# A 2112-byte pitch between the tiles of activations and gated products, and the memory's squares summed on VectorE

## The chip, the cores and the metric

The kernel runs on one core of a Trainium2 chip. The metric is the device time of one execution in microseconds; several executions are made and their median is given. A profile is one further execution, recorded instruction by instruction. The engines are TensorE (PE in the profile, with its weight loads as PEld), VectorE (DVE), ScalarE (ACT), GpSimd (POOL) and SyncE (SP, which issues most loads).

## The reference

A two-layer decoder trunk on 256 positions of width 1024 (float32). Each layer is: half-step SwiGLU, a mixer, half-step SwiGLU.

```python
def swiglu(x, w_gate, w_up, w_down):
    return (jax.nn.silu(x @ w_gate) * (x @ w_up)) @ w_down

for layer in range(2):
    if layer == 1:
        shared_kv = shared_moba_kv(h, ...)           # one key/value set, from the stream
    h = h + 0.5 * swiglu(rms_norm(h, ffn1_g), ...)   # D_FF = 2816
    hn = rms_norm(h, mix_g)
    # layer 0: 31-tap convolution module on 768 channels, layer 1: causal attention (12 heads);
    # both beside 4-head attention over a memory of 256 rows:
    mem_out = memory_attention(q_mem, rms_norm(mem, mem_g), w_mem_kv, ...)
    h = h + concat([primary, mem_out]) @ w_o
    h = h + 0.5 * swiglu(rms_norm(h, ffn2_g), ...)
```

The memory is normalized by its own root mean square, `rstd(mem)`, before its keys and values are projected.

## The kernel before

**Layout.** Activations stand transposed: 128 partitions are 128 of the 1024 (or 2816) channels, the 256 positions lie along the row. A float32 product is made of float32r parts: an activation is split into a high part and a low part, a weight as well, and of the four products three are summed: high weight by high and by low activation, low weight by high activation. The tile of split activations (`y_tiles`, pool `yp`) is `[128, 8, 2, 256]`: for each of the 8 blocks k of channels the high part and then the low part, 2048 bytes in all. The gated products `hs` (pool `hp`) are `[128, 22, 2, 256]` in the same way. So a 512-column matmul takes both parts of one k in one go with the high weight (`wh`), and a 256-column matmul takes the high part with the low weight (`wl`); `mm_run` lists these. Weights come in chunks of 1 MB, two halves each; ScalarE makes `wh` of a half (line 182), VectorE makes `wl` as raw minus `wh` (line 186), four buffers of 4096 bytes for each. One weight tile is 512 bytes of a row, so k moves on by 2048 bytes in the activations and by 512 in the weights.

**The stages.** `ffn` is called four times, with the names a, b, c, d. Its first loop runs over 22 blocks j of D_FF: gate (`ag`) and up (`au`) sums in PSUM, 32 matmuls a step in full flow, then scaling, Silu and product into `hs`. Its second loop runs over 8 blocks m of the output (`ao`, `bo`, `co`, `do`). Between them are the input projections, the attention stages, `kv` (keys and values shared by layer 1, where activations are the standing operand and `wh`, `wl` move), and the output projections `oao` and `obo`.

**The order of the work.** A scheduler places instructions; `ffn` takes a `hook(j)` that is called at the start of step j > 1 and whose instructions are kept behind the last weight split of the step before. In the first `ffn` the hook is `prepare`: at j == 5 it loads the memory `mT` and small tables, works out the rotary angles, and at its end sums the squares of the memory: `square_sum` makes the square of block k on ScalarE (`mq1` to `mq7`, two buffers) and adds it to `macc` on GpSimd (line 285), one block after another. `rstd_cols` then makes the column sums with two tiny matmuls (`rm_p`), adds epsilon on VectorE (`rm_v`) and takes the power on GpSimd (`rm_`); VectorE copies the result to `rm`. At j == 9 (`MEM_AT`) the hook scales and splits the memory (`my`, ScalarE and VectorE) and projects it (`mkv`); `rm` is used when those sums are read (`mk0t`, `mv`).

An engine takes its instructions in order, so what stands behind `rm_p` in TensorE's queue waits for it. Names in the profile are those of the tiles, with numbers left out where they repeat. A float32 matmul is recorded as two.

Of the kernel before, what the change touches and what calls it, by code (L numbers as in the profile page):

```python
# [9 lines left out]
F32 = mybir.dt.float32  # L10
F32R = mybir.dt.float32r
BF16 = mybir.dt.bfloat16
I32 = mybir.dt.int32
AF = mybir.ActivationFunctionType
ALU = mybir.AluOpType
AX = mybir.AxisListType

P = 128
DM = 1024
KD = DM // P  # L20
SEQ = 256
NT = SEQ // P
DFF = 2816
KF = DFF // P
# [26 lines left out]
MEM_AT = 9  # L51
FIRST_CAT = 3
TURN_AT = 2
Q_AT = 6
CNR_AT = 4

# [27 lines left out]
def tile_kernel(ctx: ExitStack, tc: tile.TileContext, w, xT, memT, pos, vec, hg, const, out):  # L84
    nc = tc.nc
    yp = ctx.enter_context(tc.tile_pool(name="yp", bufs=2))
    cp = ctx.enter_context(tc.tile_pool(name="cp", bufs=1))
    wp = ctx.enter_context(tc.tile_pool(name="wp", bufs=3))
    tp = ctx.enter_context(tc.tile_pool(name="tp", bufs=2))
    op = ctx.enter_context(tc.tile_pool(name="op", bufs=4))  # L90
    hp_ = ctx.enter_context(tc.tile_pool(name="hp", bufs=1))
# [8 lines left out]
    mT = cp.tile([P, KD, SEQ], F32, name="mT", tag="t8k")  # L100
# [148 lines left out]
        return ps.tile([P, 512], F32, name=name, tag=tag, bufs=bufs)  # L249


    def y_tiles(name):
        return yp.tile([P, KD, 2, SEQ], F32R, name=name, tag="y")

    def y_both(name):
        whole = yp.tile([P, KD, 2, SEQ], F32, name=name + "w", tag="y")
        return y_tiles(name), whole[:, :, 0]

    def scaled_split(y, src, k, g, on_dve=False):
# [19 lines left out]
    def square_sum(name, acc, src, first, adder=nc.gpsimd):  # L279
        if first:  # L280
            nc.scalar.activation(acc, src, AF.Square)
        else:
            sq = tp.tile([P, SEQ], F32, name=name, tag="sq")
            nc.scalar.activation(sq, src, AF.Square)
            adder.tensor_tensor(acc, acc, sq, op=ALU.add)

    def mean_cols(name, acc):

        pr = psum(name + "p", "aux", 2)
        for i in range(NT):  # L290
            mmul(pr[:, i:i + 1], acc[:, i * P:(i + 1) * P], onec, start=True, stop=True)
        v = tp.tile([P, NT], F32, name=name + "v", tag="rv")
        nc.vector.tensor_scalar(v, pr[:, :NT], EPS, None, op0=ALU.add)
        state["stat"] = state["last"]["P"]
        return v

    def rstd_cols(name, acc):
        v = mean_cols(name, acc)
        r = tp.tile([P, NT], F32, name=name, tag="rc", bufs=3)
        nc.gpsimd.tensor_tensor(r, v, mhalf[:, :NT], op=ALU.pow)  # L300
        return r
# [22 lines left out]

    def ffn(name, y, acc, nexts, store=False, both=False, hook=None, after=None, hook_down=None):

        hs = hp_.tile([P, KF, 2, SEQ], F32R, name=name + "hs", tag="hs")
        rb, first = None, acc is None
        for j in range(KF):
            if hook and j > 1:  # L330
# [3 lines left out]
            if first and j == 0:  # L334
# [12 lines left out]
                sq = cp.tile([P, KD, SEQ], F32, name="sq0", tag="kv")  # L347
                for k in range(KD):
                    nc.scalar.activation(sq[:, k], x[:, k], AF.Square)
                n = KD  # L350
# [28 lines left out]
            s = tp.tile([P, SEQ], F32, name=f"{name}s{j}", tag="s")  # L379
# [76 lines left out]
    def proj(name, y, *uses):  # L456

        os_ = [psum(f"{name}{t}") for t in range(NT)]
        n = MW * len(uses)
        if isinstance(y, tuple):  # L460
            raw = raw_chunk()
            for k in range(KD):
                for t in range(NT):
                    mmul(os_[t][:, :n], y[1][:, k, t * P:(t + 1) * P], raw[:, k * n:(k + 1) * n],
                         start=k == 0, stop=k == KD - 1)
        else:
            per = HC // n
            for k0 in range(0, KD, per):
                wh, wl = half_chunk()
                for t in range(NT):  # L470
                    for i in range(per):
                        k = k0 + i
                        mm3_tok(os_[t][:, :n], wh, wl, y, t, k, slice(i * n, (i + 1) * n), k == 0, k == KD - 1)
        for t in range(NT):
            for i, use in enumerate(uses):
                use(t, os_[t][:, i * MW:(i + 1) * MW])
# [24 lines left out]
    def values(name, r, dst, col0):  # L501
        def use(t, o):
            nc.scalar.activation(dst[:, t, col0:col0 + MW], o, AF.Copy, scale=r[:, t:t + 1])
        return use
# [110 lines left out]
    def go(head, n):  # L615
        for _ in range(n):
            next(head)

    def mem_prep(layer):
        y = y_tiles(f"my{layer}")  # L620
        for k in range(KD):
            scaled_split(y, mT[:, k], k, V_MEM + layer * KD)
        return y

    def mem_kv(layer, y, rm):
        kT = cp.tile([P, 2, SEQ], F32, name=f"mk{layer}", tag="mk")
        v = cp.tile([P, NT, MW], F32, name=f"mv{layer}", tag="mv")
        proj(f"mkv{layer}", y, keys(f"mk{layer}", rm, G_MK + layer, kT, 0, False), values(f"mv{layer}", rm, v, 0))
        return kT, v
# [58 lines left out]
    y = y_tiles("y0")  # L688
# [4 lines left out]
    def prepare(j):  # L693
        if j == MEM_AT:
            my = mem_prep(0)
            kv0.extend(mem_kv(0, my, rm))
        if j != 5:
            return
        nc.sync.dma_start(vt[:, V_TAP:], vec[:, V_TAP:])
        nc.sync.dma_start(pt, pos)  # L700
        nc.sync.dma_start(gt, hg)
        nc.sync.dma_start(mT, memT)
        nc.vector.tensor_copy(identb, ident)
        nc.vector.tensor_tensor(ident2, ident[:, :HALF_CH], ident[:, HALF_CH:], op=ALU.add)
        nc.vector.tensor_copy(maskb, cst[:, C_MASK:C_MASK + P])

        for g, n in ((G_MQ, 2), (G_Q, 1)):
            gn = gt[:, g * HD:(g + n) * HD]
            nc.vector.tensor_scalar(gn, gn, -1.0, None, op0=ALU.mult)

        posf = cp.tile([P, NT], F32, name="posf")
        nc.vector.tensor_copy(posf, pt)
        ang = cp.tile([P, NT, HALF], F32, name="ang")
        for i in range(NT):
            nc.vector.tensor_scalar(ang[:, i], cst[:, C_FREQ:C_FREQ + HALF], posf[:, i:i + 1], None, op0=ALU.mult)
        for shift, dst in ((0.25, cosT), (0.0, sinT)):
            kk = tp.tile([P, NT, HALF], F32, name="kk", tag="kk")
            nc.vector.tensor_scalar(kk, ang, 1.0 / TWO_PI, shift, op0=ALU.mult, op1=ALU.add)
            nc.vector.tensor_scalar(kk, kk, ROUND, ROUND, op0=ALU.add, op1=ALU.subtract)
            rr = tp.tile([P, NT, HALF], F32, name="rr", tag="rr")  # L720
            nc.vector.scalar_tensor_tensor(rr, kk, -PI_1, ang, op0=ALU.mult, op1=ALU.add)
            nc.vector.scalar_tensor_tensor(rr, kk, -PI_2, rr, op0=ALU.mult, op1=ALU.add)
            nc.vector.scalar_tensor_tensor(rr, kk, -PI_3, rr, op0=ALU.mult, op1=ALU.add)
            if shift:
                nc.vector.tensor_scalar(rr, rr, TWO_PI / 4, None, op0=ALU.add)
            nc.vector.tensor_scalar(rr, rr, 3.1415925, -3.1415925, op0=ALU.min, op1=ALU.max)
            nc.scalar.activation(dst[:, :, HALF:], rr, AF.Sin)
            if shift:
                nc.vector.tensor_copy(dst[:, :, :HALF], dst[:, :, HALF:])
            else:  # L730
                nc.vector.tensor_scalar(dst[:, :, :HALF], dst[:, :, HALF:], -1.0, None, op0=ALU.mult)

        macc = tp.tile([P, SEQ], F32, name="macc", tag="macc", bufs=1)
        for k in range(KD):
            square_sum(f"mq{k}", macc, mT[:, k], k == 0)
        nc.vector.tensor_copy(rm, rstd_cols("rm_", macc))

    identb = cp.tile([P, P], BF16, name="identb")
    maskb = cp.tile([P, P], BF16, name="maskb")
# [2 lines left out]
    rm = cp.tile([P, NT], F32, name="rm")  # L742
# [4 lines left out]
    def diagonals(m):  # L747
        for i in range(m * 4 * SHIFTS // KD, (m + 1) * 4 * SHIFTS // KD):
            g, s, p = i // (2 * SHIFTS), i // 2 % SHIFTS, i % 2
            nc.scalar.activation(diag[:, g, s, p * HALF_CH:(p + 1) * HALF_CH], ident2, AF.Copy,  # L750
                                 scale=vt[:, V_PP + i:V_PP + i + 1])

    (y,), acc = ffn("a", y, None, (V_MIX,), both=True, hook=prepare, after=AF.Sigmoid, hook_down=diagonals)

    hc = hp_.tile([P, KF * 2 * SEQ], F32, name="hc", tag="hs")
    hp = hc[:, :CC * (PAD + SEQ)].rearrange("p (c s) -> p c s", c=CC)
    whole = hc[:, CC * (PAD + SEQ):CC * (PAD + SEQ) + 2 * SEQ].rearrange("p (i s) -> p i s", i=2)
    cv = hc[:, KF * SEQ:KF * SEQ + CC * SEQ].rearrange("p (c s) -> p c s", c=CC)
# [151 lines left out]
    for c in range(CC):  # L910
        V(nc.vector.tensor_tensor(cv[:, c], cv[:, c], mean, op=ALU.subtract))
        sq = hp[:, c, PAD:]
# [69 lines left out]
    for k, (wh, wl, *_) in enumerate(halves):  # L982
        for m in range(KD):
            s = slice(m * P, (m + 1) * P)
# [7 lines left out]
    for m in range(KD):  # L992
        for k in range(FIRST_CAT, CC):
            mm3(o[m], next(it), cat, k, False, k == CC - 1, skip_group_check=True)
        out_end(m, o, ys, acc, V_FFN2, "oa")
    y = ys
    (ykv, y), acc = ffn("b", y, acc, (V_KV, V_FFN1 + KD))


# [11 lines left out]
    mq = qT[:, NPAIR:]  # L1011
# [14 lines left out]
    n = len(pairs)  # L1026
    for p in range(n + 1):
        if p < n:
            go(pairs[p], 1)
        if p == TURN_AT:  # L1030
            for turn in turns:
# [14 lines left out]
    y, acc = next(oproj)  # L1046
# [4 lines left out]
def _pack_weights(np_, d):  # L1051
# [20 lines left out]
    def cols(m, n=NB):  # L1072
        chunks(blocks(m, n))
# [26 lines left out]
    q = parts.pop()  # L1100
    parts.append(np_.concatenate([up[:Q_AT], q, up[Q_AT:]], axis=0))
    cols(d["w_mem_kv"][1])
# [71 lines left out]
```

## Time and profile before

| | |
|---|---|
| median of three executions | 985.27 us (983.53 to 986.44) |
| the profiled execution | 989.74 us, span 988.0 us from first to last instruction |
| mean granted clock of TensorE | 0.993 |
| TensorE busy | 973.2 us, 5788 records |
| VectorE / ScalarE / GpSimd busy | 744.2 / 599.8 / 135.7 us |
| loads from HBM | 171.43 MB, 175 GB/s over the span |

A busy time is the union of an engine's instructions. Matmuls are pipelined: each is recorded longer than the distance to the next one, so the time of one in a stream is read from start to start. The granted clock is the share of full speed at which TensorE was allowed to run. The waits list names the engine that waited, the line, and what ended the wait.

### The profile page before, as it was taken

To read this page: it belongs to the slowest core of one execution; us is meant where nothing else is said; L and a number is where in the kernel's file an instruction comes from. 1 tells how busy PE (TensorE), PEld (TensorE's weight loads), DVE (VectorE), ACT (ScalarE), POOL (GpSimd) and SP (SyncE) were. 2 spreads that over 40 slices of the span, in tenths; PEclk is the share of its full clock that TensorE was granted. 3 is DMA by queue.
4 is the path that set the end of the run, shared out by engine and by line. 5 is a ranking of instruction groups with operands and counts; after the bars stand their busy time and mean duration, and the time that the engine had idled before them with its cause. 6 is when DMAs were issued, how large, how long until landed. Compare 5 with 4: busy or idle time off the path is not lost.

```text
span 988.0 us, 15410 instructions
## 1 busy us (share of the span) xinstructions
PE 973.2 (99%) x5788; PEld 848.0 (86%) x5788; DVE 744.2 (75%) x1326; ACT 599.8 (61%) x1154; POOL 135.7 (14%) x151
## 2 busy tenths in 40 slices
PE   8899999999999999999999999999999999999998
PEld 6788888898769888888888888888996798888887
DVE  7787776679977888877766787776688588878663
ACT  6576568747667656665546656565556656565542
POOL 0502000118822100000122100000152030000000
PEclk9899999999999999999999999999998999999999
DMA  8545545543225655555555455555552056455560
GB/s 325 207 170 174 207 173 190 194 171 105 109 101 197 212 175 204 177 203 181 176 198 179 171 185 199 180 192 202 194 171 86 1 188 233 177 201 182 185 221 22
DMA packets 26427, 173.47 MB, mean 176 GB/s; under 512 B 3184, under 2 KB 4848, under 8 KB 6000
## 3 DMA queue, kind: packets, MB, share of 16 engines
q1 hardware_dynamic: 26064, 172.31, 49.7%
q8 instruction: 45, 0.74, 0.3%
q14 instruction: 30, 0.25, 0.1%
q10 hardware_dynamic: 288, 0.17, 0.1%
HBM read 171.43 MB, written 1.05 MB: 175 GB/s over the span
## 4 chain that ended last, share of the span: by engine, by line
PE 90%; ACT 3%; DVE 3%; POOL 2%; DMA 1%; issue 1%; SPq 0%; POOLq 0%; ACTq 0%; DVEq 0%
PE cg L149 7%; PE co L149 6%; PE ao L149 6%; PE do L149 6%; PE bo L149 6%; PE dg L149 6%; PE bg L149 6%; PE bu L149 6%; PE du L149 6%; PE cu L149 6%; PE ag L149 6%; PE au L149 5%; PE kv L149 3%; PE oao L149 2%; PE obo L149 2%; PE mkv L149 2%
## 5 line engine op out<-in xcount | busy, mean ns | idle before, releaser
L186 DVE TENSOR_TENSOR wl<-raw,wh 128x1024 fp32r<-128x1024 f32 (+1 forms) x310 | 377.3, 1220 | 106.5 <-ACT wh L182 99.6
L182 ACT ACTIVATE wh<-raw 128x1024 fp32r<-128x1024 f32 (+1 forms) x310 | 322.9, 1046 | 129.4 <-PE do L149 20.6
L149 PE MATMUL ag<-y,wh 128*128 128x512 f32 x176 | 48.6, 406 | 1.1 <-ACT wh L182 1.1
L149 PE MATMUL au<-y,wh 128*128 128x512 f32 x176 | 46.8, 393 | 0.0
L149 PE MATMUL co<-chs,wh 128*128 128x512 f32 (+1 forms) x198 | 45.5, 367 | 0.0
L149 PE MATMUL bo<-bhs,wh 128*128 128x512 f32 (+1 forms) x198 | 45.5, 367 | 0.0
L149 PE MATMUL do<-dhs,wh 128*128 128x512 f32 (+1 forms) x198 | 45.5, 367 | 0.0
L149 PE MATMUL ao<-ahs,wh 128*128 128x512 f32 (+1 forms) x198 | 45.4, 367 | 0.0
L149 PE MATMUL bg<-oay,wh 128*128 128x512 f32 x176 | 44.9, 393 | 0.0
L149 PE MATMUL cg<-by,wh 128*128 128x512 f32 x176 | 44.3, 393 | 0.3 <-DVE cgs L239 0.3
L149 PE MATMUL dg<-oby,wh 128*128 128x512 f32 x176 | 44.5, 393 | 0.0
L149 PE MATMUL bu<-oay,wh 128*128 128x512 f32 x176 | 44.4, 392 | 0.0
L149 PE MATMUL du<-oby,wh 128*128 128x512 f32 x176 | 44.4, 392 | 0.0
L149 PE MATMUL cu<-by,wh 128*128 128x512 f32 x176 | 44.3, 393 | 0.0
L835 POOL TENSOR_TENSOR hc<-hc,cq 128x256 f32<-128x256 f32 x58 | 42.5, 734 | 12.5 <-ACT cq L834 8.7
L843 DVE SCALAR_TENSOR_TENSOR cvp<-hc,vt,cvp 128x256 f32<-128x256 f32 x88 | 40.6, 484 | 1.5
L149 PEld LDWEIGHTS ag<-y,wh 128*128 128x128 f32 x176 | 34.1, 195 | 8.8 <-ACT wh L182 1.5
L149 PEld LDWEIGHTS ao<-ahs,wh 128*128 128x128 f32 x198 | 35.0, 189 | 5.4
L149 PEld LDWEIGHTS cg<-by,wh 128*128 128x128 f32 x176 | 32.9, 188 | 7.7 <-DVE cgs L239 0.8
L149 PEld LDWEIGHTS co<-chs,wh 128*128 128x128 f32 x198 | 35.0, 189 | 5.3
L149 PEld LDWEIGHTS bo<-bhs,wh 128*128 128x128 f32 x198 | 34.9, 189 | 5.2
L149 PEld LDWEIGHTS do<-dhs,wh 128*128 128x128 f32 x198 | 34.9, 189 | 5.2
(996 smaller groups left out, 2144.2 us busy)
## 6 DMA issues: line engine op xcount, KB each, us to landing
raw<-in_w SPq DMA_DIRECT2D x158, 1024.0 KB, 4.8
raw<-in_w SPq DMA_DIRECT2D x5, 512.0 KB, 8.3
mT<-in_memT SPq DMA_DIRECT2D x1, 1024.0 KB, 7.9
out<-x SPq DMA_DIRECT2D x8, 128.0 KB, 1.7
raw<-in_w SPq DMA_DIRECT2D x2, 256.0 KB, 4.1
x<-in_xT SPq DMA_DIRECT2D x1, 512.0 KB, 7.2
x<-in_xT SPq DMA_DIRECT2D x2, 128.0 KB, 3.3
x<-in_xT SPq DMA_DIRECT2D x1, 256.0 KB, 4.5
```

Of the source, the lines that this page charges most:

```text
L149: return in_order("P", nc.tensor.matmul(*a, **k))
L182: state["act"] = nc.scalar.activation(wh[:, s], raw[:, s], AF.Copy)
L186: state["dve"] = nc.vector.tensor_tensor(wl[:, s], raw[:, s], wh[:, s].bitcast(F32), op=ALU.subtract)
L835: state["pool"] = nc.gpsimd.tensor_tensor(cv[:, c], cv[:, c], q, op=ALU.add)
L843: nc.vector.scalar_tensor_tensor(cv[:, c] if end else o, win(c, i), tap[c][i], o, op0=ALU.mult, op1=ALU.add)
```

## The change

Three edits.

1. The tiles of activations and of `hs` get a row of 2 x 256 + 16 floats for each k, 2112 bytes, of which the first 2048 are used as before. The views that the kernel works on keep their shape.
2. The squares of the memory leave `prepare` at j == 5. At j == 7 ScalarE writes all eight into one tile (`sqm`, which takes the place in memory that `diag` uses later), and VectorE adds them as a tree: 1024, 512 and 256 columns. At j == 8 `rstd_cols` follows. `macc` is allotted earlier in the pool.
3. The DMA scratch at the start of each partition's memory is 8192 bytes instead of 16384.

```diff
+STEP = 16
@@
+    def padded(t):
+        return t[:, :, :2 * SEQ].rearrange("p k (a s) -> p k a s", a=2)
+
     def y_tiles(name):
-        return yp.tile([P, KD, 2, SEQ], F32R, name=name, tag="y")
+        return padded(yp.tile([P, KD, 2 * SEQ + STEP], F32R, name=name, tag="y"))
@@ def ffn
-        hs = hp_.tile([P, KF, 2, SEQ], F32R, name=name + "hs", tag="hs")
+        hs = padded(hp_.tile([P, KF, 2 * SEQ + STEP], F32R, name=name + "hs", tag="hs"))
@@ def prepare
+        if j == 7:
+            square_tiles()
+        if j == 8:
+            nc.vector.tensor_copy(rm, rstd_cols("rm_", macc))
         if j != 5:
             return
...
-        macc = tp.tile([P, SEQ], F32, name="macc", tag="macc", bufs=1)
+    macc = tp.tile([P, SEQ], F32, name="macc", tag="macc", bufs=1)
+
+    def square_tiles():
+        sq = cp.tile([P, KD, SEQ], F32, name="sqm", tag="kv")
         for k in range(KD):
-            square_sum(f"mq{k}", macc, mT[:, k], k == 0)
-        nc.vector.tensor_copy(rm, rstd_cols("rm_", macc))
+            nc.scalar.activation(sq[:, k], mT[:, k], AF.Square)
+        n = KD
+        while n > 1:
+            n //= 2
+            nc.vector.tensor_tensor(macc if n == 1 else sq[:, :n].rearrange("p k s -> p (k s)"), ...)
@@
-    nc = bacc.Bacc("TRN2", target_bir_lowering=False, num_devices=1)
+    nc = bacc.Bacc("TRN2", target_bir_lowering=False, num_devices=1, dynamic_dma_scratch_size=8192)
```

On TensorE, in the first `ffn`, `rm_p` stood between the up sum of step 4 (`au_408`) and the gate sum of step 5 (`ag_531`):

```order
L149 MATMUL au_408<-y_116,wl_1_432 128x256 x8
L149 MATMUL au_408<-y_116,wh_1_431 128x512 x8
L149 MATMUL rm_p<-onec,macc 128x1 x2
L149 MATMUL ag_531<-y_116,wh_0_535 128x512 x8
L149 MATMUL ag_531<-y_116,wl_0_536 128x256 x8
```

Now two further steps, `ag_501`/`au_502` and `ag_559`/`au_560`, stand ahead of it (line numbers are one higher):

```order
L150 MATMUL au_502<-y_116,wh_1_525 128x512 x8
L150 MATMUL ag_559<-y_116,wh_0_563 128x512 x8
L150 MATMUL ag_559<-y_116,wl_0_564 128x256 x8
L150 MATMUL au_560<-y_116,wl_1_584 128x256 x8
L150 MATMUL au_560<-y_116,wh_1_583 128x512 x8
L150 MATMUL rm_p<-onec,macc 128x1 x2
L150 MATMUL ag_629<-y_116,wh_0_633 128x512 x8
```

It has moved by eight rows, two steps of gate and up; the matmuls around it are the same.

On VectorE, before, `rm_v` (which reads `rm_p`) came between two weight splits of step 6, and nothing of the squares was there:

```order
L382 TENSOR_TENSOR ah_344<-ah_344,as_340 128x256
L384 TENSOR_TENSOR ahs<-ah_285,ahs 128x256
L378 TENSOR_TENSOR ags_395<-ags_395,anb 128x256
L726 TENSOR_SCALAR rr<-rr 128x16
L239 TENSOR_TENSOR ags_453<-ag_407,ags4c 128x256
L731 TENSOR_SCALAR sinT<-sinT 128x2x8
L293 TENSOR_SCALAR rm_v<-rm_p 128x2
L186 TENSOR_TENSOR wl_1_614<-raw_591,wh_1_613 128x1024
```

Now the tree of additions (`sqm`, `macc`) stands there, with the splits for step 7 (`wl_0_634`, `wl_1_654`) between its parts, and `rm_v` follows eight rows further on:

```order
L382 TENSOR_TENSOR ags_454<-ags_454,anb 128x256
L750 TENSOR_TENSOR sqm<-sqm 128x1024
L386 TENSOR_TENSOR ah_403<-ah_403,as_399 128x256
L739 TENSOR_SCALAR sinT<-sinT 128x2x8
L187 TENSOR_TENSOR wl_0_634<-raw_631,wh_0_633 128x1024
L750 TENSOR_TENSOR sqm<-sqm 128x512
L388 TENSOR_TENSOR ahs<-ah_345,ahs 128x256
L240 TENSOR_TENSOR ags_547<-ag_501,ags5c 128x256
L737 COPY cosT<-cosT 128x2x8
L187 TENSOR_TENSOR wl_1_654<-raw_631,wh_1_653 128x1024
L750 TENSOR_TENSOR macc<-sqm 128x256
```

Three additions are new in VectorE's queue; the seven on GpSimd (`macc<-macc,mq`) are gone from its own. After the memory's projection the engines' orders are the same as before but for two rows on ScalarE in the attention of layer 1.

More of the change, by code (lines that the diff above doesn't have):

```diff
@@ L249, in psum @@
         return ps.tile([P, 512], F32, name=name, tag=tag, bufs=bufs)
+    def padded(t):
+        return t[:, :, :2 * SEQ].rearrange("p k (a s) -> p k a s", a=2)
     def y_tiles(name):
-        return yp.tile([P, KD, 2, SEQ], F32R, name=name, tag="y")
+        return padded(yp.tile([P, KD, 2 * SEQ + STEP], F32R, name=name, tag="y"))
     def y_both(name):
-        whole = yp.tile([P, KD, 2, SEQ], F32, name=name + "w", tag="y")
+        whole = padded(yp.tile([P, KD, 2 * SEQ + STEP], F32, name=name + "w", tag="y"))
         return y_tiles(name), whole[:, :, 0]
@@ L731, in prepare @@
                 nc.vector.tensor_scalar(dst[:, :, :HALF], dst[:, :, HALF:], -1.0, None, op0=ALU.mult)
-        macc = tp.tile([P, SEQ], F32, name="macc", tag="macc", bufs=1)
+    macc = tp.tile([P, SEQ], F32, name="macc", tag="macc", bufs=1)
+    def square_tiles():
+        sq = cp.tile([P, KD, SEQ], F32, name="sqm", tag="kv")
         for k in range(KD):
-            square_sum(f"mq{k}", macc, mT[:, k], k == 0)
-        nc.vector.tensor_copy(rm, rstd_cols("rm_", macc))
+            nc.scalar.activation(sq[:, k], mT[:, k], AF.Square)
+        n = KD
+        while n > 1:
+            n //= 2
+            nc.vector.tensor_tensor(macc if n == 1 else sq[:, :n].rearrange("p k s -> p (k s)"),
+                                    sq[:, :n].rearrange("p k s -> p (k s)"),
+                                    sq[:, n:2 * n].rearrange("p k s -> p (k s)"), op=ALU.add)
     identb = cp.tile([P, P], BF16, name="identb")
@@ L753, in tile_kernel @@
     (y,), acc = ffn("a", y, None, (V_MIX,), both=True, hook=prepare, after=AF.Sigmoid, hook_down=diagonals)
-    hc = hp_.tile([P, KF * 2 * SEQ], F32, name="hc", tag="hs")
+    hc = hp_.tile([P, KF * (2 * SEQ + STEP)], F32, name="hc", tag="hs")
     hp = hc[:, :CC * (PAD + SEQ)].rearrange("p (c s) -> p c s", c=CC)
```

## The prediction

> **What bounds the kernel now.** I read the page first (engine shares, slices, chain), then the waits, then the stretch of time in which TensorE's clock drops, then the spacing of equal matmuls.
>
> ```profile
> span 988.0 us, 15410 instructions
> PE 973.2 (99%) x5788; PEld 848.0 (86%) x5788; DVE 744.2 (75%) x1326; ACT 599.8 (61%) x1154; POOL 135.7 (14%) x151
> PEclk9899999999999999999999999999998999999999
> PE 90%; ACT 3%; DVE 3%; POOL 2%; DMA 1%; issue 1%; SPq 0%; POOLq 0%; ACTq 0%; DVEq 0%
> ```
>
> TensorE is busy 99% of the span and is 90% of the chain of work that ended last. So two things can change the time: a stretch in which TensorE waits or runs at a lower clock, and the time of one matmul. The clock row shows two slices below 9 (the second of 40 and the one at three quarters); the second slice holds the largest wait of TensorE:
>
> ```profile
> PE rm_p L149 <- POOL macc L285: 4.2, 1, 4.2
> L285 POOL TENSOR_TENSOR macc<-macc,mq x7: 735/1167/2888, 27.3 to 37.8; 128x256 f32<-128x256 f32 x7
> 34.60 2.01 PE L149 MATMUL au<-y,wh 128*128 128x512 f32 x8
> 40.77 1.01 PE L149 MATMUL rm_p<-onec,macc 128*128 128x1 f32 x4 [4.16 <-POOL macc L285]
> 41.64:49.81 8.17, 8.17 (x33) 0.66 0.37 130
> 49.81:55.37 5.56, 5.56 (x34) 1.00 0.36 115
> 55.37:60.92 5.55, 5.55 (x33) 1.00 0.48 155
> ```
>
> Rows are: wait (engine and line waited for, total, times, longest); the tile `macc` with its shortest, median and longest addition in ns; two rows of the timeline (start, us); and stretches (from:to, length, TensorE busy, granted clock, DMA share, GB/s). The seven GpSimd additions take up to 2.9 us each, TensorE stands still 4.16 us for the last one, and the whole gate-and-up step behind it (`ag5`, `au5`) runs at a granted clock of 0.66 and takes 8.17 us, where the next two take 5.56 and 5.55 at 1.00.
>
> For the time of a matmul I take rows of the timeline in full flow, where one row is a run of equal matmuls and the next row's start ends it:
>
> ```profile
> 339.24 1.07 PE L149 MATMUL bu<-oay,wl 128*128 128x256 f32 x8
> 340.15 1.07 PE L149 MATMUL bg<-oay,wl 128*128 128x256 f32 x8
> 341.05 1.99 PE L149 MATMUL bg<-oay,wh 128*128 128x512 f32 x8
> 342.88 1.99 PE L149 MATMUL bu<-oay,wh 128*128 128x512 f32 x8
> 344.71 1.10 PE L149 MATMUL bu<-oay,wl 128*128 128x256 f32 x8
> 345.65 1.10 PE L149 MATMUL bg<-oay,wl 128*128 128x256 f32 x8
> 346.60 2.00 PE L149 MATMUL bg<-oay,wh 128*128 128x512 f32 x8
> ...
> 453.84 2.00 PE L149 MATMUL bo<-bhs,wh 128*128 128x512 f32 x8
> 455.68 1.60 PE L149 MATMUL bo<-bhs,wl 128*128 128x256 f32 x12
> 457.11 3.82 PE L149 MATMUL bo<-bhs,wh 128*128 128x512 f32 x16
> 460.76 1.36 PE L149 MATMUL bo<-bhs,wl 128*128 128x256 f32 x10
> 523.71 10.73 PE kv L149 x46
> ```
>
> From start to start, a 256-column matmul on `oay` takes 113 ns in one step (340.15 to 341.05, eight) and 118 ns in the next (344.71 to 345.65); on `bhs` it takes 119 ns (455.68 to 457.11, twelve). A 512-column one takes 229 ns on `oay` (1.83 us for eight), 228 ns on `bhs` (3.65 us for sixteen), and 233 ns in `kv`, where weights move and activations stand (10.73 us for 46). Same shape, same clock of 1.00: so the place of the operands, or the phase between a matmul and the load of the next weights, is worth up to 7 ns of 113 and 5 ns of 228. That is what a pitch can touch.
>
> **The change part by part.** The durations come from the profiled execution, which took 989.74 us (span 988.0), 4.5 us or 0.45% above the median of 985.27. The sum is made against its own time and then set against the median.
>
> *Squares of the memory.* Removed: seven GpSimd additions and the dependence of `rm_p` on them. `rm_p` now stands two steps later, ahead of `ag7`. What goes is the wait of 4.16, the clock's loss of 8.17 - 5.55 = 2.62, and what `rm_p` itself lost: it lasted 0.87 (40.77 to 41.64), the same four small matmuls elsewhere 0.36:
>
> ```profile
> 23.28 0.50 PE L149 MATMUL anrp<-onec,aacc 128*128 128x1 f32 x4
> 23.64 1.63 PE L149 MATMUL au<-y,wh 128*128 128x512 f32 x6
> L353 DVE TENSOR_TENSOR sq<-sq x2: 686/954/1221, 15.8 to 18.1; 128x1024 f32<-128x1024 f32 x1, 128x512 f32<-128x512 f32 x1
> L353 DVE TENSOR_TENSOR aacc<-sq x1: 421/421/421, 19.9 to 19.9; 128x256 f32<-128x256 f32 x1
> sum 33.12, PE 28.96 PEld 25.17 DVE 27.48 ACT 20.30 POOL 11.50; mean PE 7.24 PEld 6.29 DVE 6.87 ACT 5.08 POOL 2.88
> 56.80 3.30 ACT L275 ACTIVATE my<-mT,vt 128x256 fp32r<-128x256 f32 x8
> 61.91 1.22 DVE L186 TENSOR_TENSOR wl<-raw,wh 128x1024 fp32r<-128x1024 f32 x1
> 66.41 0.39 PE L149 MATMUL mkv<-wh,my 128*128 128x512 f32 x1
> ```
>
> Together 4.16 + 2.62 + 0.51 = 7.3 us less.
>
> Added: three VectorE additions of 1024, 512 and 256 columns. The same tree for x took 1.22 + 0.69 + 0.42 = 2.33 us. The eight squares stay on ScalarE, now in one piece; the eight activations of `my`, the same shape, took 3.30 us in one piece at 56.8 without TensorE waiting, so I cost that at nothing. If its cover, the low and high halves already made, were gone, it would cost at most those 3.3 us.
>
> How much of the 2.33 us shows is open. The `sum` row covers 27.80 to 60.92: VectorE was busy 27.5 of 33.1 us. Without the 7.3 us TensorE wants the same work in 25.8, and VectorE has 27.5 + 2.3 = 29.8. The 4 us that are missing come out of its lead. The half of `wl` for the first `mkv` matmul was done at 63.1 and wanted at 66.4 (a lead of 3.3), and VectorE had idle time ahead of it. Laid out by these durations, in the new order, VectorE works (an estimate) without a gap from 36 us on, finishes `macc` at about 47.6 where TensorE reaches `rm_p` at 47.4, and reaches the halves for `mkv` between 0 and 2 us ahead of need. Behind `rm_p` in TensorE's queue stands `ag7`, so a late `macc` stops everything; behind `rm_v` on VectorE stand a `wl` of `au8` and the low part of `my`. I take 0.3 us of wait at `rm_p` and 0.3 at `mkv`; ends 0 and 3.3 (the lead gone twice over would still be under the 4.16 seen). This part: 7.3 - 0.6 = 6.7 us less.
>
> *GpSimd, and what waits for `rm`.* With the additions gone nothing on GpSimd is late. `rm` was copied at 44.1 us and is first read by `mk0t` at 76.4; now it is copied some 53 us into the span (behind the `wl` that follows `rm_v`) and read near 69, so 16 us of other work still cover it. No load on SP's queue is moved.
>
> ```profile
> L736 DVE COPY rm<-rm__528 x1: 165/165/165, 44.1 to 44.1; 128x2 f32<-128x2 f32 x1
> L481 ACT ACTIVATE mk0t<-mkv,rm x2: 473/475/477, 76.4 to 77.8; 128x256 f32<-128x256 f32 x2
> ```
>
> *Pitch and addresses.* No instruction is added. Up to now the distance from a moving tile to its weights is the same modulo 512 bytes for every k (2048 against 512 a step); then it moves on by 64 bytes a step and goes through all eight values. No row shows such a stream, so I bound it by the rows above. Counts: 1408 matmuls of each width in the gate and up steps, 616 of 512 and 880 of 256 columns in the down steps, some 190 and 620 elsewhere (`kv`, `mkv`; `obo`, `oao`, `bq`, `ca`, `cg`, `mq`):
>
> ```profile
> L149 PE MATMUL bg<-oay,wh 128*128 128x512 f32 x176 | 44.9, 393 | 0.0
> L149 PE MATMUL bg<-oay,wl 128*128 128x256 f32 x176 | 24.4, 279 | 0.0
> L149 PE MATMUL bo<-bhs,wh 128*128 128x512 f32 x154 | 37.7, 391 | 0.0
> L149 PE MATMUL bo<-bhs,wl 128*128 128x256 f32 x176 | 27.0, 283 | 0.0
> 223.54 3.45 PE ca L149 x16
> ```
>
> If every matmul took the fastest value seen (113 and 228): gate and up 1408 x (115.5 - 113) + 1408 x 1 = 4.9, down 880 x 6 = 5.3, the rest 190 x 5 + 620 x 5 = 4.0, in all 14 us less. If every one took the slowest (120 rounded up, and 233): 1408 x 4.5 + 1408 x 4 + 616 x 5 + 620 x 2 = 16 us more. If instead the streams visit all seen values alike, 256 columns cost (113 + 118 + 119) / 3 = 117 and 512 columns 230: gate and up 3.5 more, down 880 x 2 less and 616 x 2 more, the rest 1.2 less, about +2. I take 0, between this and the gain that the steadily slow 119 ns of the down steps invites, and keep -14 and +16. [...]
>
> [...]
>
> *DMA scratch of 8 KB.* No DMA is issued from GpSimd in the order of instructions, before or after, so nothing waits for the scratch. It makes room and moves every tile's address, the effect of which is inside the bounds of the pitch. Nothing by itself.
>
> **Sum**: 989.7 - 6.7 + 0 = 983.0 us for an execution like the profiled one; 4.5 less, 985.3 - 6.7 = 978.6 us, for the median.
>
> **The rivals.**
> 1. *The pitch helps.* A changing distance breaks the slow locked state of the down steps and more. For it: both quoted rows there run at 119 ns, against 113 elsewhere. [...]
> 2. *The pitch hurts* (the other side). A constant distance lets a stream settle: `bhs` runs its sixteen at 228 but the eight between two switches at 230. If the distance changes at every step the stream never settles. Each ns on all 5100 matmuls costs 5.1 us, so from 1.3 ns on the gain of the squares is used up, from 1.9 ns on the kernel is slower by 0.3%; at the upper bound 978.6 + 16 = 995.
> 3. *The wait only moves.* `macc`, now behind 1.2 + 0.7 + 0.4 us of additions between the `wl` halves in VectorE's queue, is late at `ag7`, or VectorE's lead breaks at `mkv`, and the clock falls again. With 2 to 4 us of wait and a second clock loss of 2.6: 983 to 985. Against it: two steps of 5.55 us of room.
>
> **How the numbers follow.** 0.3% (3 us) is about what a measurement here can tell from no change: faster is below 982.3, slower above 988.2. Main case (stall gone, pitch within 4 us): 0.48, 978.6, by itself 974.5 to 982.5. Rival 1: 0.22, 950 to 974.5. Rival 2: 0.18, of which 0.09 ends between 982.5 and 988, 0.09 above. Rival 3: 0.12, of which 0.03 still faster, 0.07 the same, 0.02 slower. Faster 0.47 + 0.22 + 0.03 = 0.72, same 0.17, slower 0.11. The range 963 to 990 leaves out about 0.07 below (towards the 216 ns row) and 0.09 above.
>
> **What would show it.** Right: no wait of TensorE for `macc` above 1 us, clock 1.00 in the second slice of the page, gate and up steps of 5.55 us throughout, `rm_p` ahead of `ag7`. The pitch is read from the start-to-start of the rows quoted: 113 to 118 and 229 in gate and up, 119 and 228 in down, if it does nothing; 113 and below, or 120 and 233 and above, if it does. Wrong: a wait at `rm_p` or `mkv` followed by a clock below 1.00, or a step other than 5.45 to 5.65 us, which over 88 steps moves the end by more than 8 us.

## The result, and the profile after

| | before | after |
|---|---|---|
| median | 985.27 us (982.1 to 991.6, five executions) | 990.71 us (990.04 to 992.65, five executions) |
| profiled execution, span | 989.74, 988.0 us | 992.65, 990.9 us |

The ratio is 1.0066, 95% interval 1.0041 to 1.0092: the change makes the kernel about 0.7% slower. The forecast was 978.6.

The page of the changed kernel, the rows that were shown of before (span; engines; granted clock in 40 slices; share of the chain that ended last):

```profile
span 990.9 us, 15395 instructions
PE 979.1 (99%) x5788; PEld 848.3 (86%) x5788; DVE 744.0 (75%) x1329; ACT 600.8 (61%) x1154; POOL 125.6 (13%) x144
PEclk9999999999999999999999999999997999999999
PE 92%; ACT 3%; DVE 2%; POOL 2%; DMA 1%; issue 1%; POOLq 0%; ACTq 0%; DVEq 0%
```

The 8 in the second slice is gone, so the stall was removed. The slice at three quarters fell from 8 to 7. TensorE is busy 5.9 us longer (979.1 against 973.2) with the same 5788 records. Its granted clock was not lower (0.995 against 0.993 on average), so the matmuls themselves take longer.

TensorE's three longest waits, and the place of `rm_p` (timeline: start, us):

```profile
PE ab2s L150 <- ACT q1T L457: 1.8, 1, 1.8
PE pw L108 <- DVE onec L110: 1.5, 1, 1.5
PE am10pp L153 <- ACT am11p L568: 1.3, 1, 1.3
```

```profile
45.42 2.03 PE L150 MATMUL au<-y,wh 128*128 128x512 f32 x8
47.29 0.50 PE L150 MATMUL rm_p<-onec,macc 128*128 128x1 f32 x4
47.65 2.09 PE L150 MATMUL ag<-y,wh 128*128 128x512 f32 x8
58.94 0.39 PE L150 MATMUL mkv<-wh,my 128*128 128x512 f32 x1
```

`rm_p` has no wait behind it in brackets, takes its 0.36 us, and `mkv` starts at 58.94 where it started at 66.41: 7.5 us gained on that execution. The steady stream, though, reads otherwise:

```profile
340.94 2.03 PE L150 MATMUL bg<-oay,wh 128*128 128x512 f32 x8
342.80 2.02 PE L150 MATMUL bu<-oay,wh 128*128 128x512 f32 x8
344.66 1.10 PE L150 MATMUL bu<-oay,wl 128*128 128x256 f32 x8
345.60 1.11 PE L150 MATMUL bg<-oay,wl 128*128 128x256 f32 x8
346.54 2.03 PE L150 MATMUL bg<-oay,wh 128*128 128x512 f32 x8
...
451.62 1.57 PE L150 MATMUL bo<-bhs,wl 128*128 128x256 f32 x12
453.02 3.87 PE L150 MATMUL bo<-bhs,wh 128*128 128x512 f32 x16
456.73 1.34 PE L150 MATMUL bo<-bhs,wl 128*128 128x256 f32 x10
```

Eight 512-column matmuls on `oay` take 1.86 us, 232.5 ns each (before 229); the 256-column ones 118 (before 113 in one step, 118 in the next). A step takes 5.60 us (340.94 to 346.54; before 5.55 at 118, from 341.05 to 346.60, and less at 113). From `bg` to `bo`, 22 steps and what stands beside them, it is 125.28 us where it was 123.50: 0.08 us a step, 7 us over 88. On `bhs` 512 columns take 232 ns (before 228), 256 columns 117 (before 119).

Where the 2.9 us between the two spans went, by the start of the same tiles in both traces (after minus before, us):

| first matmul of | mkv | ao | bg | bo | kv | co | am10pp | ab2s | ab0pp | dg | do |
|---|---|---|---|---|---|---|---|---|---|---|---|
| | -7.5 | -6.5 | -5.9 | -4.1 | -3.9 | -2.4 | -1.7 | -0.7 | +0.8 | +0.8 | +2.7 |

Three things move: -7.5 at `rm_p`, +2.6 in the attention of layer 1 (`am10pp` to `ab0pp`), and what is left, 2.9 + 7.5 - 2.6 = +7.8, spread over all streams. The attention of layer 1, in stretches of time (columns: from:to, length, busy of PE, PEld, DVE, ACT, POOL, granted clock, DMA share, GB/s), after and then before:

```profile
756.00:759.00 3.00, 1.25 (x12) 1.01 (x11) 1.96 (x8) 2.75 (x11) 0.00 (x0) 1.00 0.00 0
759.00:763.00 4.00, 4.00 (x21) 1.86 (x20) 1.15 (x4) 0.16 (x1) 0.00 (x0) 0.57 0.00 0
```

```profile
757.00:760.00 3.00, 2.05 (x17) 1.81 (x18) 2.28 (x8) 2.60 (x11) 0.00 (x0) 0.98 0.00 0
760.00:763.00 3.00, 3.00 (x26) 1.76 (x24) 1.78 (x8) 1.31 (x5) 0.00 (x0) 1.00 0.00 0
```

TensorE has more idle time ahead of `ab2s` (the scores of the next pair of heads), and then runs at a clock of 0.57 (0.51 from 759.3 to 762.7). This is a second stretch at half clock: both traces also have one of 6.83 us at 0.50 just before (from 750.3 to 757.1 us before, from 749.0 to 755.8 after). The longer idle time has its cause on ScalarE, which copies the queries that `ab2s` reads into `q1T` (timeline of after, then of before):

```profile
757.77 0.49 ACT L568 ACTIVATE ab1p<-ab1s,ab1n 128x256 f32<-128x256 f32 x1
758.13 0.22 ACT L568 ACTIVATION_READ_ACCUMULATOR ab1p<-ab1s,ab1n 128x1 f32 x1
758.22 0.68 ACT L457 ACTIVATE q1T<-bq2p 128x256 f32<-128x256 f32 x2
```

```profile
758.98 0.66 ACT L453 ACTIVATE q1T<-bq2p 128x256 f32<-128x256 f32 x2
759.51 0.39 ACT L564 ACTIVATE ab1p<-ab1s,ab1n 128x128 f32<-128x128 f32 x1
```

Before, the two copies of `q1T` stood between the two pairs of exponentials (`ab1p`); now they stand behind both. `ab2s` waits for them, 1.75 us in place of 0.95. These are the "two rows on ScalarE" of the text on the change. The half-clock stretch behind the wait is not what a usual execution of the changed kernel has: the profiled one was the slowest of the five, with a mean granted clock of 0.995. The other four had 0.998, which is some 3 to 5 us at half clock in all (an estimate from these figures and the span of 989 us).

### The profile page after: what moved, and what is told of

Its sections match the earlier page's. It is cut to its first block, busy times and chain, and to the rows that moved or that the text cites. A ratio compares the mean times of both kernels' runs of the same rounds, so it can differ in the third digit from the quotient of the medians.

```text
span 990.9 us, 15395 instructions
## 1 busy us (share of the span) xinstructions
PE 979.1 (99%) x5788; PEld 848.3 (86%) x5788; DVE 744.0 (75%) x1329; ACT 600.8 (61%) x1154; POOL 125.6 (13%) x144
## 4 chain that ended last, share of the span: by engine, by line
PE 92%; ACT 3%; DVE 2%; POOL 2%; DMA 1%; issue 1%; POOLq 0%; ACTq 0%; DVEq 0%
PE cg L150 7%; PE dg L150 6%; PE bg L150 6%; PE bu L150 6%; PE ao L150 6%; PE do L150 6%; PE co L150 6%; PE bo L150 6%; PE du L150 6%; PE cu L150 6%; PE au L150 6%; PE ag L150 6%; PE kv L150 3%; PE oao L150 2%; PE obo L150 2%; PE mkv L150 2%
```

## The experiments

All times are medians. Each ratio is to the kernel before, run on the same chip beside it (median 984.4 us for the first eight, 985.7 for the last four); ratio and interval come from all executions, so a ratio can differ by 0.001 from that of the two medians.

### The three edits one by one

The squares alone, on the old pitch and scratch (the `prepare` and `square_tiles` hunks of the diff):

> The kernel before with the squares moved alone; pitch 2048 and scratch as before. Theory A (the changing distance between moving tile and weights slows every matmul stream, the squares do gain): steps of gate and up stay at 5.53 to 5.56 us, the wait of 4.2 us at rm_p is gone, 978 to 982 us. Rival B (the loss comes from the squares: in the new order ScalarE makes q1T two instructions later in the attention of layer 1, TensorE waits longer there and a second stretch at half clock follows): 985 us or more, steps unchanged. Rival C (the addresses, moved by the smaller scratch): like A here.

Measured: 982.83 us, ratio 0.9989 (0.9980 to 0.9998). That is far less than 7.5, and lies between the 978 to 982 of theory A and the 985 of rival B. In its profile the copies of `q1T` stand behind the exponentials too, so the swap comes with this edit and not with the pitch. Relative to the profile of before it is 7.1 us ahead at `bq` (the queries of layer 1) and 4.7 from `ab0pp` on. But this profile is the slowest of its eleven executions (985.08 us, granted clock 0.994, where seven had 0.998 and two 1.0), so the half-clock stretch that is part of this loss is not usual either; the 0.8 us of longer wait are what the new order adds.

The pitch and the smaller scratch, with the old squares:

> The kernel before with the pitch of 2112 bytes and the scratch of 8 KB; squares as before. Theory A: steps of gate and up at 5.60 to 5.62 us instead of 5.53, down stages 0.2 us longer, 512 columns at 232 ns in both, 993 to 997 us. Rival B: 984 to 987 us. Rival C: 993 to 997 us as A.

Measured: 992.39 us, ratio 1.0091 (1.0072 to 1.0110). The loss is here, just under the 993 to 997 of theory A; from `bg` to `bo` its trace has 125.30 us, as after. Rival C expected the same, so it takes the next run to tell the pitch from the scratch.

The scratch alone:

```diff
-    nc = bacc.Bacc("TRN2", target_bir_lowering=False, num_devices=1)
+    nc = bacc.Bacc("TRN2", target_bir_lowering=False, num_devices=1, dynamic_dma_scratch_size=8192)
```

> The kernel before with the scratch of 8 KB alone: every tile 8192 bytes lower, all distances as before. Theory A and rival B: 984 to 987 us, steps of 5.53 us. Rival C: 990 us or more.

Measured: 983.28 us, ratio 0.9995 (0.9986 to 1.0004): nothing, and the median is a little under the 984 to 987 expected. So rival C is out. The ratio of the squares and that of pitch and scratch together multiply to 1.0080, inside the interval of the whole change. This kernel has the order of instructions of before, so its profile is a second execution of the old stall:

```profile
L285 POOL TENSOR_TENSOR macc<-macc,mq x7: 735/797/1757, 27.4 to 36.3; 128x256 f32<-128x256 f32 x7
```

```profile
38.11 0.61 PE L149 MATMUL rm_p<-onec,macc 128*128 128x1 f32 x4 [1.77 <-POOL macc L285]
```

The median addition took 0.80 us, not 1.17, the longest 1.76, not 2.89; the wait was 1.77 us, not 4.16; and no slice of its clock row is below 9. The copies of `q1T` stand in their old place, and layer 1 has no half-clock stretch at all. Seven kernels in all kept the old squares and were profiled beside the kernel before:

| | seven additions, us | wait at `rm_p` | half clock behind it |
|---|---|---|---|
| before | 10.4 | 4.16 | 6.83 |
| scratch alone | 7.6 | 1.77 | none |
| pitch and scratch | 8.0 | 1.69 | 3.41 |
| weights moved, 0 and 192 (below) | 8.0 | 1.81 | 3.41 |
| pitch 2112 in the activations alone | 7.6 | 1.70 | 3.41 |
| pitch 2560 in the activations | 6.6 | 0.40, then 1.40 behind it | 3.41 |
| pitch 2112 in the gated products alone | 6.6 | 0.42, then 1.41 behind it | none |
| weights at 128 (below) | 6.6 | 0.30, then 1.40 behind it | 3.41 |

So the profiled execution of before was the worst of these eight. The usual stall is 1.7 to 1.8 us in all. Behind it there are 3.41 us at half clock, which cost a further 1.7, or none: about 2 to 3.5 us together (an estimate from these rows). The longer wait at `ab2s` takes 0.8 of that back, which leaves 1 to 3 us for the squares; 1.1 was measured by the ratio (0.2 to 2.0), and 1.6 between the medians.

The half-clock stretches of the table last 3.41 or 6.83 us. Waits of 1.69 to 1.81 us are followed by such a stretch in three kernels of the table, and by none in the one with the scratch alone, at 1.77. What decides between the two, no run shows.

### What the pitch does: streams at a held distance

A small kernel that does none of the trunk's work: streams of 48 matmuls, each on float32r operands as in the kernel, nothing beside them, one profiled execution. The distance is the address of the moving operand minus that of its weights within a partition.

```diff
+    for i in range(8):
+        stream("full_" + letters[i], 512, 16 * i)
+    for i in range(8):
+        stream("half_" + letters[i], 256, 16 * i)
+    stream("full_pa", 512, 0, pitch=528)
...
+    stream("full_pb", 512, 0, pitch=640)
...
```

The third argument is the offset in floats, so stream i of the first eight holds the distance at 64 x i bytes for every k. A pitch of 528 floats (2112 bytes) changes the distance with k; one of 640 (2560 bytes) holds it modulo 256.

> Not the reference: streams of 48 float32r matmuls by themselves, 512 or 256 columns, each with a new weight tile 512 bytes further on; the output is the input x with a few columns overwritten. The distance from moving tile to weights, modulo 512 bytes, is held at 0, 64, ... 448 (full_a to full_h, half_a to half_h), or it changes by 64 bytes a matmul (full_pa, half_pa, pitch 2112), or not at all at pitch 2560 (full_pb, half_pb). Theory A: held distances settle at 226 to 233 ns (512 columns) and 113 to 120 (256), different ones for different distances; the changing distance gives 231 to 233 and 118; pitch 2560 gives the values of full_a and half_a; the pairs full_wb, full_wd, which move both tiles by the same amount, give those of full_a. Rival: the distance does not matter, then all eight agree within 1 ns and pa too.

Timeline of TensorE (one row a stream; the next row's start ends it):

```profile
20.42 11.04 PE L106 MATMUL full_a<-mv,wt 128*128 128x512 f32 x48
31.30 11.17 PE L106 MATMUL full_b<-mv,wt 128*128 128x512 f32 x48
42.30 11.32 PE L106 MATMUL full_c<-mv,wt 128*128 128x512 f32 x48
53.46 11.36 PE L106 MATMUL full_d<-mv,wt 128*128 128x512 f32 x48
64.66 11.06 PE L106 MATMUL full_e<-mv,wt 128*128 128x512 f32 x48
...
108.92 5.91 PE L106 MATMUL half_a<-mv,wt 128*128 128x256 f32 x48
114.67 5.82 PE L106 MATMUL half_b<-mv,wt 128*128 128x256 f32 x48
120.33 5.86 PE L106 MATMUL half_c<-mv,wt 128*128 128x256 f32 x48
126.02 5.63 PE L106 MATMUL half_d<-mv,wt 128*128 128x256 f32 x48
131.49 5.90 PE L106 MATMUL half_e<-mv,wt 128*128 128x256 f32 x48
...
154.06 11.28 PE L106 MATMUL full_pa<-mv,wt 128*128 128x512 f32 x48
165.18 5.80 PE L106 MATMUL half_pa<-mv,wt 128*128 128x256 f32 x48
170.82 11.08 PE L106 MATMUL full_pb<-mv,wt 128*128 128x512 f32 x48
181.74 5.91 PE L106 MATMUL half_pb<-mv,wt 128*128 128x256 f32 x48
```

`full_a` takes 10.88 us (20.42 to 31.30), 226.7 ns a matmul; `full_d` 11.20, 233.3. The mean distance of the last 24 starts of each stream, in ns:

| distance, bytes | 0 | 64 | 128 | 192 | 256 | pitch 2112 | pitch 2560 |
|---|---|---|---|---|---|---|---|
| 512 columns | 226.7 | 228.9 | 232.3 | 233.3 | 226.7 | 231.7 | 226.7 |
| 256 columns | 120.0 | 117.8 | 118.7 | 113.3 | 120.0 | 117.5 | 120.0 |
| sum of both | 346.7 | 346.7 | 351.0 | 346.7 | 346.7 | 349.2 | 346.7 |

In these streams, once settled, the time depends on the distance modulo 256 bytes: 320, 384 and 448 gave the same as 64, 128 and 192 (48 matmuls of 512 columns took 11.00, 11.16 and 11.20 us in both). Moving weights and activations together by 64 or 192 bytes gave, once settled, the values of distance 0 (the whole streams took 10.93 and 10.90 us for 512 columns, against 10.88, and 5.75 for 256 columns in all three), so the distance counts and not the address. The built programs tell where the kernel stands. Before, `y` lies at distance 64 from `wh` and `wl`, and its rows of 229 and 118 ns agree with the stream; the 113 ns of every other step do not. `hs` lies at 0, with 228 and 119 ns near the stream's 226.7 and 120. In `kv`, where the weights move, the distance is 192, and the 233 ns that the prediction read there are the stream's 233.3. With 2112 bytes the distance grows by 64 from k to k (2112 - 2048; 512 a step in the weights is a multiple of 256), visits all four values, and 512 columns cost 231.7, near the mean of the four (230.3) and above it.

### Can a better distance be held?

The weight buffers moved apart, so that the high weights are at distance 0 and the low weights at 192, the fastest value for each. The scratch is 8 KB, here and in all runs below but the last; it was worth nothing by itself.

```diff
+    gap = ctx.enter_context(tc.tile_pool(name="gap", bufs=1))
+    gap.tile([P, 16], F32, name="gap0")
     op = ctx.enter_context(tc.tile_pool(name="op", bufs=4))
...
+    gap1.tile([P, 16], F32, name="gap1")
+    lp = ctx.enter_context(tc.tile_pool(name="lp", bufs=4))
...
+    gap2.tile([P, 48], F32, name="gap2")
...
-        wl = op.tile([P, HC], F32R, name=f"wl{n}_{h}", tag="wl", bufs=4)
+        wl = lp.tile([P, HC], F32R, name=f"wl{n}_{h}", tag="wl", bufs=4)
```

> The kernel before with 8 KB of scratch and the old pitch of 2048 bytes, but the weight buffers moved: the distance from the moving operand to the weights, modulo 256 bytes, is held at 0 for the high weights and at 192 for the low ones, in the activations and in the gated products. Before it is 64 in the activations and 0 in the gated products, for both weights. Theory (the distance alone sets the time of a matmul, as in the streams of the experiment before): gate and up steps 16 x (226.7 + 113.3) ns = 5.44 us in place of 5.53, 88 steps, so -8 us; the low-weight matmuls of the down projections 113.3 in place of 118 to 120 ns, about 704 of them, so -4 to -5; the rest -1. Median 971 (969 to 974). Rival (streams without other traffic don't carry over; loads, splits and other engines' accesses decide): steps 5.5 to 5.6 us and 983 +- 2.

Measured: 985.45 us, ratio 1.0011 (1.0001 to 1.0020). The expected 13 us did not come. Timeline:

```profile
342.65 2.00 PE L156 MATMUL bg<-oay,wh 128*128 128x512 f32 x8
344.49 1.97 PE L156 MATMUL bu<-oay,wh 128*128 128x512 f32 x8
346.30 1.10 PE L156 MATMUL bu<-oay,wl 128*128 128x256 f32 x8
347.25 1.11 PE L156 MATMUL bg<-oay,wl 128*128 128x256 f32 x8
348.19 2.00 PE L156 MATMUL bg<-oay,wh 128*128 128x512 f32 x8
```

`bu` on `wh` came down to 226 ns (1.81 us), but `bg`, the first after a switch from `wl`, still takes 230, and the narrow ones 118, not 113.3. From `bg` to `bo` it is 123.89 us (before 123.50), while a down stage takes 61.19 (before 61.52): four times 0.33 gained, 88 steps of 0.02 lost, together nothing. So for the wide matmuls the streams carry over, and for the narrow ones they do not.

The single starts show more. In this run the wide matmuls of `bg` lie 233, 236, 228, 233 and 231 ns apart before they settle at 226 or 227. The same shows in the down steps of before, where eight in a row take 230 and sixteen 228.4: over 226.7, both make 27 ns, lost once behind each switch (an estimate from these rows). The narrow ones do not settle at the stream's value. In the stream `half_d` they lie 118, 120, 119, 124 and 118 ns apart and only then 113 or 114 for good. Here all sixteen in a row, both with the low weights at 192, lie 117 to 120 apart and none reaches 113. And before, at 64, the sixteen of one step lie 113 to 114 apart from the first on, those of the next 117 to 119. So a run of narrow matmuls holds one of two rhythms at one distance. What picks it, no run shows.

The same with the squares on VectorE, and then with the copies of `q1T` put ahead of all exponentials:

> The same, and the memory's squares on VectorE as in the changed kernel. Theory: the squares edit is worth what it was by itself (ratio 0.9989, so 1 us less than with the weight buffers moved alone): 970 (968 to 973). Rival (in a faster flow the wait for the GpSimd sums is longer, since those do not get faster): 2 to 5 us less than with the buffers alone. Rival (distances do not carry over): 982.

Measured: 983.29 us, ratio 0.9997 (0.9987 to 1.0007); about 2 us less than without the squares edit. The expected 970 missed as in the run before; the rival that distances do not carry over, 982, came nearest.

```diff
-        nc.scalar.activation(dst[:, pair0:pair0 + 2, t * P:(t + 1) * P],
-                             pp[:, :2 * P].rearrange("p (a b) -> p a b", a=2), AF.Copy)
+        i = nc.scalar.activation(dst[:, pair0:pair0 + 2, t * P:(t + 1) * P],
+                                 pp[:, :2 * P].rearrange("p (a b) -> p a b", a=2), AF.Copy)
+        if name.startswith("bq2"):
+            in_order("A", i)
```

> The same as the last, with the two copies of q1T of layer 1 fixed ahead of the exponentials in ScalarE's order. Theory (the order of these copies made the wait at ab2s longer): the wait at ab2s 0.95 us or less in place of 1.7, and no stretch of half clock after it, 1 to 3 us less than without: 968 (966 to 971). Rival (the wait is set elsewhere, by the ranking): same time as without, 970.

Measured: 981.77 us, ratio 0.9980 (0.9972 to 0.9989), 1.5 us less than without the reordering, within the 1 to 3 expected; the absolute 968 missed as before. From the list of waits, without and with it:

```profile
PE ab2s L156 <- ACT q1T L460: 1.8, 1, 1.8
```

```profile
PE ab2s L156 <- ACT q1T L460: 0.3, 1, 0.3
```

The 1.8 us became 0.3, which is the whole 1.5 between the medians. The half-clock stretch of 3.41 us that begins 0.6 us after `ab2s` in the trace without the reordering is gone too, but that trace is of the slowest of its twelve executions (986.26 us).

### The pitch itself, or the distance?

A pitch of 2560 bytes in the activations, which keeps the distance modulo 256:

```diff
+STEP = 128
...
-        return yp.tile([P, KD, 2, SEQ], F32R, name=name, tag="y")
+        return padded(yp.tile([P, KD, 2 * SEQ + STEP], F32R, name=name, tag="y"))
```

> A pitch of 2560 bytes in the activations alone (gated products at 2048), 8 KB of scratch, the squares as before. The step of 512 bytes from k to k in the weights and of 2560 in the activations leaves the distance modulo 256 the same for every k. Theory (a distance that changes with k costs, a pitch by itself does not): gate and up steps 5.53 us as before and 983 +- 2. Rival (any pitch other than 2048 costs, by the way that the reads fall on the memory): steps 5.6 us and 989 to 990.

Measured: 984.42 us, ratio 1.0000 (0.9991 to 1.0009). So a wider pitch alone costs nothing; the rows read 229 and 113 to 118 as before.

The opposite: the pitch of 2048 kept, two gaps (48 floats ahead of the weights, 32 ahead of `hs`) hold the distance at 128 everywhere:

> The pitch of 2048 bytes kept, squares as before, 8 KB of scratch; two gaps put weights, activations and gated products so that the distance from moving operand to weights is held at 128 modulo 256 everywhere (before: 64 in the activations, 0 in the gated products). Theory (the distance sets the time, the pitch only through it; 128 was the slowest of the four in the streams: 232.3 + 118.7 ns against 228.9 + 117.8): steps 5.60 to 5.62 us, +6 to +8, the down stages +1 to +2, so 992 (989 to 994) with no pitch changed at all. Rival (only a distance that changes from k to k costs): steps 5.53 us, 984 +- 1.5.

Measured: 996.93 us, ratio 1.0105 (1.0084 to 1.0126), slower than the changed kernel without any change of pitch.

```profile
340.76 2.02 PE L153 MATMUL bg<-oay,wh 128*128 128x512 f32 x8
342.62 2.02 PE L153 MATMUL bu<-oay,wh 128*128 128x512 f32 x8
344.48 1.11 PE L153 MATMUL bu<-oay,wl 128*128 128x256 f32 x8
345.43 1.11 PE L153 MATMUL bg<-oay,wl 128*128 128x256 f32 x8
346.38 2.03 PE L153 MATMUL bg<-oay,wh 128*128 128x512 f32 x8
```

The step takes 5.62 us, 512 columns 232.5 ns and 256 columns 118.8, as in the stream at 128. The median is 3 us above the range expected; from `bg` to `bo` it is 125.65 us (before 123.50), 2.15 for 22 steps and so 8.6 for 88, and the down stage behind it 0.4 longer than before, 1.6 for four. That makes 10.2 of the 11. So a distance held at 128 costs at least as much as one that changes (996.93 against the 992.39 us of pitch and scratch).

Then the pitch of 2112 in one of the two places each:

> The pitch of 2112 bytes in the activations alone, 8 KB of scratch, squares as before. Theory (distances that change with k cost 3 to 5 ns of a 512-column and up to 4 ns of a 256-column matmul): steps of gate and up 5.60 us in place of 5.53, 88 of them, +6.3; about 990.5 (989 to 992). Rival (the gated products carry the cost): 984.5.

Measured: 992.91 us, ratio 1.0061 (1.0036 to 1.0085), 0.9 us above the range expected; from `bg` to `bo` 125.28 us, as in the changed kernel.

> The pitch of 2112 bytes in the gated products alone, 8 KB of scratch, squares as before. Theory: the down stages take 61.7 us in place of 61.55, four of them, so +0.7: 985 (984 to 986.5); 512 columns 3 to 4 ns slower, 256 columns 1 to 2 ns faster. Rival (the gated products carry the cost of the change): 990.

Measured: 985.81 us, ratio 0.9997 (0.9985 to 1.0009). Its `bo` rows read 231 and 117 ns like those of after, and cost 0.2 us a stage. So the activations carry the loss. (The two ratios multiply to less than the 1.0091 of both places together, but the intervals overlap.) In the activations there is one 512-column matmul for each of 256, and the old distance of 64 had the low ones at 113 in half the steps; in the gated products, the 2 ns that 880 narrow matmuls gain nearly pay for the 4 that 616 wide ones lose.

### A faster version

The squares on VectorE and the copies of `q1T` ahead of the exponentials; pitch, weights and scratch as before:

> The kernel before with the memory's squares on VectorE and with the two copies of q1T of layer 1 ahead of the exponentials in ScalarE's order; pitch 2048, weights where they were. Theory (the weights' new places in the run with all three were worth nothing): 981.8 (981 to 983). Rival (they were worth the 1 to 2 us): 983.

Measured: 981.90 us, ratio 0.9956 (0.9938 to 0.9974). The version with moved weights had 0.9980 against the kernel before beside it, so the moved weights gained nothing. This one is faster than both kernels of this case.

## Why the prediction was wrong, point by point

**The pitch, taken as 0, measured +9 us (ratio 1.0091, together with the scratch, which is worth nothing).** This term decided it. Its bounds were -14 and +16, its rows and counts were right, and so was, for the wide matmuls, the reading that the place of the operands sets the 228 and 233 ns; for the narrow ones the kernel showed both 113 and 118 at the one distance of 64. The step that failed is the choice between the ends. It averaged what the rows happened to show (113, 118 and 119; 228, 229 and 233), which gave +2, and rounded that to 0 for a gain hoped for in the down steps. The streams show the four values that a changing distance visits, with a mean of 230.3 and 117.5 ns, and 231.7 and 117.5 measured under the changing distance; the kernel's gate and up steps have 232 to 233 and 118. For 1408 pairs, 3.5 ns more on 512 columns and 2.5 more on 256 make 8 us. The second rival had the direction and the price: from 1.9 ns a matmul on the kernel is slower. Its reason, that a constant distance lets a stream settle, is only half of it, since the kernel is as slow with the distance held at 128 (1.0105). The sign to look for was in the profile: `kv` at 233 and `hs` at 228 with the same shape show places that differ by 5 ns, and the old place of the activations, 229 and 113 to 118, had the lowest sum of all rows shown, so that a change had more to lose than to win there.

The chances of the first rival reach down to 950, the time that 216 ns for every 512-column matmul would give (3.45 / 16 us, the row of `ca`, plain float and 256 columns). No run shows a float32r one at 216: the fastest stream takes 226.7 ns, and the fastest kernel has a median of 981.77 us. In the streams one shape takes 226.7 to 233.3 ns in one program, by the distance of the two operands alone; why, no run shows.

**The squares, taken as -7.3, measured -1.** Against the profiled execution the term was right: 7.3 forecast, and `mkv` starts 7.5 us earlier. But that execution was 4.5 us above the median; the prediction said so and still took the whole stall off the median. Much of the excess lay in that very stall: the same additions let TensorE wait 1.8 us in other executions, 4.16 in that one. Against the profile of the run with the scratch alone it lost 5.6 us up to `mkv` and 1.7 more at the half-clock stretch of layer 1. The term was mis-sized by reading a time that varies from one execution; it is 2 to 3.5 us.

**What is late next: taken as 0.6 us at `rm_p` and `mkv`, measured 0 there, and 2.6 in layer 1 in the profiled execution.** `macc` was ready sooner than laid out: its last addition starts at 45.00 and takes 0.42, against an estimated end of 47.6. The third rival did not happen in the place it named. It happened 700 us later, at `ab2s`, by the two swapped rows on ScalarE, which the text on the change listed and the sum left without a price: a copy that TensorE waits for moved behind two more exponentials. That is 0.8 us of wait, and in the profiled execution, the slowest of five, a half-clock stretch as well.

**The scratch, taken as nothing: right** (0.9995). **`rm` covered: right**; it is copied at 51.6 us and first read at 68.9. **Clock 1.00 in the second slice, `rm_p` ahead of `ag7`, no wait for `macc`: right.** **Gate and up steps of 5.55 us: wrong**, 5.60; the wide matmuls take the 233 ns announced for a pitch that hurts, the narrow ones 118 and not 120. But 5.60 lies inside the 5.45 to 5.65 that the prediction still called right, and 5.55 was itself the slower of two steps that alternated before: that sign was too wide for a loss of 7 us.

## What to carry to other kernels

Before a tile gets another pitch, look up what that does to the distance from the moving operand to its weights. Here a distance (modulo 256 bytes) held at 128 everywhere, or changing in the activations, cost 0.6 to 1.1%, while the other kernels with moved tiles stayed within 0.1% of before. With TensorE busy 99% of the span, 3.5 ns more on each of 1408 wide matmuls and 2.5 more on each of 1408 narrow ones, 8 us, outweighed a stall of 2 to 3.5 us. Before a stall is costed, ask whether the profiled execution is a usual one: one that lies well above the median may be so because of that very stall. The same question goes to the profile of the changed kernel, which here was the slowest of five. And price every row that a scheduler moves, even far from the edit, if TensorE waits for it.

## What the runs showed of the hardware

- In the streams a float32r matmul of 512 columns takes 226.7, 228.9, 232.3 or 233.3 ns and one of 256 columns 120.0, 117.8, 118.7 or 113.3 ns from start to start, by the distance of moving operand and weights at 0, 64, 128 or 192 bytes modulo 256; finer offsets of 16 and 32 bytes give 231.7 and 233.3, and 116.7 for both. Nothing else ran beside them. The wide one is fastest at 0, where the narrow one is slowest, and three of the four distances have the same sum.
- Some of these streams took five to nine matmuls to settle (narrow ones at 192 bytes: 118 to 124 ns for five, then 113; wide ones moved with their weights by 64 bytes: 224 to 236 for nine, then 226 or 227). In the kernel before, at a distance of 64, sixteen narrow ones in a row hold 113 ns in one step and 118 in the next.
- The same seven GpSimd additions took 6.6 to 10.4 us in eight executions, and the wait for them 0.3 to 4.2.
